# Layer 0's feed-forward in seven block products, and its modulation reductions moved into the two mixers

## The chip, the cores and the metric

One core of one Trainium2 chip runs the whole program. The metric is the time of one execution in microseconds on the device. Beside the runs that are only timed there is one profiled execution, from which every row below is taken.

## The reference, cut to what matters

Two transformer layers work on 640 tokens of 1024 features: 512 tokens of a sample and 128 of a prompt, each with its own modulation. A layer is a mixer and a gated feed-forward, both behind a normalisation that is scaled and shifted by the modulation:

```python
sh, sc, gt, shf, scf, gtf = adaln(silu(c) @ ada_w[layer] + ada_b[layer])   # 6 chunks of 1024, for c and for c_ctx
x = x + gt * mixer(rmsnorm(x) * (1 + sc) + sh)
h = rmsnorm(x) * (1 + scf) + shf
x = x + gtf * ((silu(h @ w_gate) * (h @ w_up)) @ w_down)                   # d_ff = 2816 = 22 slabs of 128
```

Mixer 0 is an S5 recurrence beside neighbourhood attention (four pairs of heads); mixer 1 is a bidirectional Mamba-2 (SSD) in four groups of heads. Everything is in float32.

## The kernel before, in words

A tile framework orders the instructions: every engine and the DMA queue of SyncE (SP) runs its own list in order; the order follows the program's text, with an instruction that could not run yet stepping back behind those that can. SBUF is mostly an arena of twelve blocks (`blk`), two large blocks (`big`), and a weight pool with three slots each of `whi` and `wlo` and two of `wraw`. Matrix products accumulate in PSUM: two double banks `acc` and four single banks `pm`.

A float32 matrix is multiplied as three products of rounded halves. `load_w` (L263) brings a slab of 128 output features over SP's queue, ScalarE rounds it to `whi` (L186), VectorE makes the rest `wlo` (L187), and `gemm` (L278) issues, per 128 inputs, whi by xh, whi by xl and wlo by xh, each in two halves of 320 or 322 columns (L290).

**The modulation** has 96 slabs of 128 features (48 for each layer, 8 to each of the six chunks). The first five chunks of layer 0 are computed on TensorE by `ada_unit` (L218): four steps, each of two 512 KB loads into a `whi` and a `wlo` slot and four float32 matmuls with a stationary tile of 32 columns and 512 moving columns, side by side in the four column groups of the array (two instructions each in the trace). All four steps add into one `pm` bank; then a copy on ScalarE, four transposes and two small additions on VectorE follow. Chunks 2, 3 and 4 of layer 0 run inside mixer 0's attention (`ada_fill`, L1304). The other 56 slabs (chunk 5 of layer 0 and all of layer 1) are computed on VectorE by `ada_tile` (L241): a 512 KB load over SP into a ring of five slots (`adar`, a large block) and two reductions over 1024 elements for each slab (L246), placed in layer 0's feed-forward by `fill` in `build`, two or three slabs for every slab f of gate and up.

**The feed-forward of layer 0** is `ffn` (L393): parts of 8, 7 and 7 slabs. For each f, one gemm of gate and one of up (96 matmuls of 322 columns), the scaling by the row norm (L366), SiLU and product, and the rounding of the result; at a part's end eight gemms with `w_down`, whose result is added to x (`residual`, L381). After the last part's slab m the next norm's work for x[m] follows (`norm_tile`, L335).

**The feed-forward of layer 1** is `ffn_blocks` (L503): parts of 4, 6, 6 and 6. In the first part the products are the plain gemms, and beside them `token_forms` (L433) makes seven combinations of halves of the normalised tokens, rounded in two pieces (`fm`, seven blocks). From f = 4 on, `block_pair` (L460) computes gate and up together from seven products of 128 x 512 weight combinations with those forms: 7 x 4 x 3 = 84 matmuls of 320 columns (L482) for each f.

**Mixer 0's end** (`even_mixer`, L1415): while the fourth pair of heads is in `attention(3)`, the generators `s5_out` (L1182) and `glu` (L1229) are advanced step by step. For each of four feature slabs b, `s5_out` loads `wraw<-kd`, `whi<-fd` and `wlo<-fd`, runs 48 small matmuls, transposes, copies on VectorE to `s5yT`, and a GELU that goes ScalarE, VectorE (L1223), ScalarE, VectorE (L1225), and is rounded to `gh` and `gl`. `glu` is four gemms on those; then the eight gemms with `ev_w_out` follow in `build`.

**Mixer 1** (`odd_mixer`, L901): for each group g, `ssd_group` (L723) yields fourteen times, and `weave` (L846) advances the gemms of the next group (or, in group 3, `ssd_partial`) between them by the digits of `steps`. Nearly every small product of `ssd_group` takes a `pm` bank.

Of the kernel before, what the change touches and what calls it, by code (L numbers as in the profile page):

```python
# [25 lines left out]
FF_PARTS = ((0, 8), (8, 15), (15, 22))  # L26
# [38 lines left out]
def lay_out(a):  # L65
# [5 lines left out]
    d["ada_n"] = np.ascontiguousarray(w[:, :, :5120].reshape(8, 128, 5, 1024).transpose(2, 0, 1, 3))  # L71
    d["cond"] = np.ascontiguousarray(np.broadcast_to(np.stack([a["c"][0], a["c_ctx"]])[None], (128, 2, 1024)))
    d["vecs"] = np.concatenate([fmajor(a[n]) for n, _ in VECS], 1)
    d["ada_w"] = np.ascontiguousarray(a["ada_w"].transpose(0, 2, 1).reshape(96, 128, 1024)[40:])
# [45 lines left out]
class Kernel:  # L120
# [97 lines left out]
    def ada_unit(self, u, pair, row):  # L218
# [16 lines left out]
        m = self.mod[0][:, 8 * u:8 * u + 8].rearrange("p (b j) s -> p b j s", b=2)  # L235
        v = self.vec("ada_b")[:, 8 * u:8 * u + 8].rearrange("p (b j) -> p b j", b=2)
# [12 lines left out]
    def ada(self, layer, tiles):  # L249
        nc = self.nc  # L250
        for j in tiles:
            w = self.adar[:, self.adai % 5]
            self.adai += 1
            nc.sync.dma_start(w, self.I["ada_w"][layer * 48 + j - 40])
            self.ada_tile(layer, j, w)
            if j % 8 == 7:
                self.ada_bias(layer, j - 7, j + 1)
# [135 lines left out]
    def ffn(self, layer, fill=None, after=None):  # L393
        nc = self.nc
        gate = self.mod[layer][:, 40:48]
        for f0, f1 in FF_PARTS:
            nf = f1 - f0
            hh = self.blks("hh", 2, [4, T], F32R)
            hl = self.blks("hl", 2, [4, T], F32R)
            ht = lambda k: (hh[k // 4][:, k % 4], hl[k // 4][:, k % 4])  # L400
            for f in range(f0, f1):
                if fill:
                    fill(f)
                wg = self.load_w(self.I["ffn_w_gate"][layer * NFF + f], 8)
                pg = self.gemm(wg, self.xt, 8, GH)
                wu = self.load_w(self.I["ffn_w_up"][layer * NFF + f], 8)
                pu = self.gemm(wu, self.xt, 8, GH)
                wk = self.blk("ffw", [BLK])
                tg = self.scaled(wk[:, :G], pg)
                tu = self.scaled(wk[:, G:2 * G], pu)  # L410
                sg, hd = wk[:, 2 * G:2 * G + T], wk[:, 2 * G + T:2 * G + 2 * T]
                for s, (a, b, d) in enumerate(SEGS):
                    nc.scalar.activation(sg[:, a:b], tg[:, d:d + b - a], AF.Silu, bias=tg[:, NS + s:NS + s + 1])
                    nc.vector.scalar_tensor_tensor(hd[:, a:b], tu[:, d:d + b - a], tu[:, NS + s:NS + s + 1],
                                                   sg[:, a:b], op0=OP.add, op1=OP.mult)
                self.split(*ht(f - f0), hd)
            last = f1 == NFF
            if last and after is None:
                self.ffn_end(layer, f0, nf, ht)
                return  # L420
            if last:
                after[0]()
            for m in range(8):
                wd = self.load_w(self.I["ffn_w_down"][layer * 8 + m][:, f0 * 128:f1 * 128], nf)
                pd = self.gemm(wd, ht, nf, TH)
                self.residual(self.xk(m), pd, m, gate)
                if last:
                    after[1](m, self.xk(m))
            if last:
                after[2]()  # L430

# [71 lines left out]
    def ffn_blocks(self, layer):  # L503
# [6 lines left out]
        for f0, f1 in ((0, 4), (4, 10), (10, 16), (16, NFF)):  # L510
# [25 lines left out]
            if f1 == NFF:  # L536
                self.ffn_end(layer, f0, nf, ht)
                return
            for m in range(8):
# [1017 lines left out]
```

## Time and profile before

| | us |
|---|---|
| median of 3 runs | 1922.17 (1919.78 to 1922.27) |
| the profiled execution, its own time | 1922.12 |
| its span in the trace | 1920.3 |
| TensorE busy | 1837.2 (96% of the span) |
| VectorE busy | 1342.8 (70%) |
| ScalarE busy | 818.7 (43%) |
| GpSimd busy | 369.6 (19%) |

The profiled execution's own time is 1.8 us above its span, and 0.05 us below the median. The mean granted clock of TensorE over the span is 0.979 of full speed. Matmuls are pipelined: the mean duration of one (some 310 ns for 320 columns) is longer than the distance between two, so distances and windows are the measure of what one costs.

### The profile page before, as it was taken

Reading aid. Unit: us, or ns where it says so; the run is one execution under the profiler, and the core shown is the slowest. Engines: PE = TensorE matmul, PEld = TensorE weight load, DVE = VectorE, ACT = ScalarE, POOL = GpSimd, SP = SyncE. Lnnn points to the kernel's source line nnn. Section 1 sums busy time; section 2 is a strip of 40 time slices with the busy share of each in tenths; the row PEclk is TensorE's granted clock in tenths of the full one; section 3 lists DMA queues with packets and bytes.
Section 4 is the critical chain, followed back from the end, with each engine's and each line's share of the span. In section 5 each row is a group of like instructions: output and inputs, shape, how many; then the busy total and the mean of one; then the engine's idle time right before and its main releaser. Section 6 shows DMA issues by size and latency. Waiting matters only on the chain.

```text
span 1920.3 us, 30941 instructions
## 1 busy us (share of the span) xinstructions
PE 1837.2 (96%) x12340; PEld 1710.7 (89%) x12340; DVE 1342.8 (70%) x2255; ACT 818.7 (43%) x1374; POOL 369.6 (19%) x425
## 2 busy tenths in 40 slices
PE   4899999899999999999999999998999999999997
PEld 1887778899999999999998788875799999999997
DVE  7879933568846856876778696878646876574764
ACT  5454344542212222234655465655444644252442
POOL 1029800010000000012023534346523000000002
PEclk8899999999999999999999999999899999999999
DMA  7355355525434534433221212123422132222222
GB/s 293 119 143 179 114 162 143 216 88 169 156 98 136 163 119 133 157 101 99 93 66 61 77 61 83 57 76 106 134 108 78 39 105 77 82 84 77 94 69 80
DMA packets 102144, 215.82 MB, mean 112 GB/s; under 512 B 15072, under 2 KB 50544, under 8 KB 101488
## 3 DMA queue, kind: packets, MB, share of 16 engines
q1 hardware_dynamic: 101968, 213.83, 34.5%
q8 instruction: 97, 1.59, 0.4%
q14 instruction: 47, 0.39, 0.1%
q0 software_dynamic: 32, 0.02, 0.0%
HBM read 192.31 MB, written 18.84 MB: 110 GB/s over the span
## 4 chain that ended last, share of the span: by engine, by line
PE 82%; DVE 4%; ACT 1%; issue 1%; DMA 1%; DVEq 0%; SPq 0%; ACTq 0%
PE acc L290 59%; PE acc L482 8%; PE pm L482 3%; PE acc L564 1%; PE pm L738 1%; PE pm L564 1%; PE pm L820 1%; DVE ssdw L794 1%; PE pm L1205 1%; PE pm L805 1%; PE pm L787 1%; DVE cv L671 1%; PE acc L1386 1%; PE pm L824 1%; PE pm L226 1%
## 5 line engine op out<-in xcount | busy, mean ns | idle before, releaser
L290 PE MATMUL acc<-xh,whi 128*128 128x322 f32 (+1 forms) x1744 | 417.7, 319 | 8.4 <-ACT xh L1280 6.2
L290 PE MATMUL acc<-xl,whi 128*128 128x322 f32 (+1 forms) x1744 | 416.5, 317 | 0.0
L290 PE MATMUL acc<-xh,wlo 128*128 128x322 f32 (+1 forms) x1744 | 415.9, 317 | 0.0
L186 ACT ACTIVATE whi<-wraw 128x1024 fp32r<-128x1024 f32 (+3 forms) x202 | 204.0, 1011 | 489.1 <-PE acc L290 322.3
L290 PEld LDWEIGHTS acc<-xh,whi 128*128 128x128 f32 x1744 | 296.4, 190 | 24.6 <-issue 14.3
L290 PEld LDWEIGHTS acc<-xh,wlo 128*128 128x128 f32 x1744 | 296.2, 190 | 11.1 <-issue 10.6
L290 PEld LDWEIGHTS acc<-xl,whi 128*128 128x128 f32 x1744 | 297.5, 190 | 8.4 <-issue 7.9
L182 POOL TENSOR_TENSOR ssq<-ssq 128x640 f32<-128x640 f32 (+2 forms) x45 | 71.0, 1577 | 1095.7 <-DMA wraw<-in_ffn_w_down 438.3
L187 DVE TENSOR_TENSOR wlo<-wraw,whi 128x1024 fp32r<-128x1024 f32 (+3 forms) x202 | 242.6, 1202 | 33.0 <-ACT whi L186 32.5
L381 DVE SCALAR_TENSOR_TENSOR x<-acc,mod,x 128x320 f32<-128x320 f32 x168 | 63.4, 434 | 131.3 <-PE acc L290 131.1
L246 DVE CUSTOM_DVE_ANT_0 junk<-adar,cond 128x1024 bf16<-128x1024 f32 x112 | 136.8, 1221 | 1.8
L482 PE MATMUL acc<-fm,whi 128*128 128x320 f32 x576 | 127.5, 309 | 0.0
L671 DVE SCALAR_TENSOR_TENSOR cv<-cv,vecs 128x644 f32<-128x644 f32 x96 | 97.8, 1019 | 15.4 <-ACT cv L669 13.8
L482 PEld LDWEIGHTS acc<-fm,whi 128*128 128x128 f32 x576 | 96.2, 188 | 0.1
L482 PE MATMUL acc<-fm,wlo 128*128 128x320 f32 x288 | 88.8, 309 | 0.0
L290 PE MATMUL acc<-hh,wlo 128*128 128x320 f32 x352 | 79.9, 309 | 0.0
L290 PE MATMUL acc<-hl,whi 128*128 128x320 f32 x352 | 79.8, 308 | 0.0
L290 PE MATMUL acc<-hh,whi 128*128 128x320 f32 x352 | 79.8, 309 | 0.0
L290 PE MATMUL acc<-hb,whi 128*128 128x320 f32 x384 | 72.3, 310 | 2.3 <-DVE fsc L182 1.2
L366 DVE TENSOR_TENSOR ffw<-acc,rext 128x644 f32<-128x644 f32 x52 | 43.1, 828 | 39.2 <-PE acc L290 37.6
L794 DVE SCALAR_TENSOR_TENSOR ssdw<-ssdw,dtk,ssdcb 128x128 f32<-128x128 f32 x160 | 60.4, 441 | 11.2 <-ACT ssdw L792 11.0
L182 POOL TENSOR_TENSOR mt<-s5x,s5co 128x128 f32<-128x128 f32 x79 | 41.7, 537 | 119.3 <-DMA s5x<-in_s5h 114.4
(394 smaller groups left out, 3628.9 us busy)
## 6 DMA issues: line engine op xcount, KB each, us to landing
adar<-in_ada_w SPq DMA_DIRECT2D x56, 512.0 KB, 4.1
wraw<-in_ffn_w_gate SPq DMA_DIRECT2D x44, 512.0 KB, 3.2
wraw<-in_ffn_w_up SPq DMA_DIRECT2D x44, 512.0 KB, 3.3
wraw<-in_od_w_in SPq DMA_DIRECT2D x40, 512.0 KB, 3.2
wraw<-in_ffn_w_down SPq DMA_DIRECT2D x24, 384.0 KB, 3.2
wraw<-in_ev_w_in SPq DMA_DIRECT2D x16, 512.0 KB, 4.1
wraw<-in_od_w_out SPq DMA_DIRECT2D x16, 512.0 KB, 3.6
wlo<-in_ada_n SPq DMA_DIRECT2D x15, 512.0 KB, 5.0
```

Of the source, the lines that this page charges most:

```text
L182: e.tensor_tensor(o, a, b, op=op)
L186: self.nc.scalar.activation(hi, x, AF.Copy)
L187: self.nc.vector.tensor_tensor(lo, x, hi.bitcast(F32), op=OP.subtract)
L226: nc.tensor.matmul(ps[q:q + 32], self.condf[:, 2 * i + a], w[a][:, b * 512:b * 512 + 512], start=i == 0, stop=i == 3)
L246: nc.vector.tensor_tensor_reduce(out=junk, in0=w, in1=self.cond[:, s], scale=1.0, scalar=0.0, op0=OP.mult, op1=OP.add, accum_out=self.mod[ ...
L290: nc.tensor.matmul(ps[:mw, h, :n], a[:, k, :mw], b[:, h * n:(h + 1) * n], start=k0 + k == 0 and q == 0, stop=k0 + k == total - 1 and q == 2)
L366: self.nc.vector.tensor_tensor(t.rearrange("p (h n) -> p h n", h=2), ps[:, :, :GH], self.rext.rearrange("p (h n) -> p h n", h=2), op=OP.mult)
L381: nc.vector.scalar_tensor_tensor(xk[:, a:b], pv, gate[:, m, s:s + 1], xk[:, a:b], op0=OP.mult, op1=OP.add)
L482: nc.tensor.matmul(ps, m[:, k0 + k], x[:, k], start=first and k == 0 and q == 0, stop=k == 3 and q == 2, skip_group_check=not first)
L564: nc.tensor.matmul(ps[:, :n], w[:, k], x[:, a:b], start=k == 0 and q == 0, stop=k == nf - 1 and q == 2)
L671: nc.vector.scalar_tensor_tensor(acc, cb[:, k:k + G], cw[:, k * 24 + wi:k * 24 + wi + 1], acc, op0=OP.mult, op1=OP.add)
L794: nc.vector.scalar_tensor_tensor(E[:, h], E[:, h], self.dt[:, 0, c, g * 8 + h:g * 8 + h + 1], cbs, op0=OP.mult, op1=OP.mult)
```

## The change

The feed-forward of layer 0 becomes `ffn_blocks` too; `ffn` is gone. `ffn_blocks` takes over the `after` hooks (the next norm). The modulation slabs leave the feed-forward: chunk 5 of layer 0 and chunk 0 of layer 1 (16 slabs) go to VectorE during `attention(3)` and `s5_out`, with a ring of two slots in an arena block and with `load_cond` moved there; chunk 1 of layer 1 (8 slabs) goes to VectorE beside the eight gemms with `ev_w_out`, one slab each; chunks 2 to 5 of layer 1 (four units of four steps) go to TensorE in mixer 1's groups 1 to 3.

```diff
-FF_PARTS = ((0, 8), (8, 15), (15, 22))
+FF_PARTS = ((0, 4), (4, 10), (10, 16), (16, 22))
...
-            w = self.adar[:, self.adai % 5]
+            w = self.adar[:, self.adai % self.adar.shape[1]]
...
-    def ffn(self, layer, fill=None, after=None):
...
-    def ffn_blocks(self, layer):
+    def ffn_blocks(self, layer, after=None):
...
+            last = f1 == NFF
+            if last and after is None:
                 self.ffn_end(layer, f0, nf, ht)
                 return
+            if last:
+                after[0]()
             for m in range(8):
                 w = self.load_w(self.I["ffn_w_down"][layer * 8 + m][:, f0 * 128:f1 * 128], nf)
                 self.residual(self.xk(m), self.gemm(w, ht, nf, TH), m, gate)
+                if last:
+                    after[1](m, self.xk(m))
+            if last:
+                after[2]()
...
+        fill = self.ada_fill((3, 4, 2, 5), 1)
+
+        def with_fill(main, at):
+            for i, _ in enumerate(main):
+                if i in at:
+                    next(fill, None)
+                yield
+
         for g in range(4):
             nxt = [self.ssd_in(g + 1)] if g < 3 else [self.ssd_partial()]
-            self.weave(self.ssd_group(g), *([self.ssd_z(g)] if g else []), *nxt, steps=('11111111111112', '11211111111111', '12111111001111', '12011111111101')[g])
+            self.weave(with_fill(self.ssd_group(g), ((), (2, 6, 10), (1, 3, 5, 7, 9, 11), (1, 2, 3, 4, 5, 7, 9))[g]), *([self.ssd_z(g)] if g else []), *nxt, steps=('11111111111112', '11211111111111', '12111111001111', '12011111111101')[g])
+        for _ in fill:
+            pass
...
-        self.af = af = self.blk("af", [4, T])
+        self.af = af = self.blk("af", [3, T])
...
-        fill = self.ada_fill()
+        fill = self.ada_fill((2, 3, 4))
...
         for i, _ in enumerate(self.attention(3)):
             if i < 3:
                 self.split(ah[:, i], al[:, i], af[:, i])
+            if i == 3:
+                self.load_cond()
+                self.adar, self.adai = self.blk("adar", [2, 1024]), 0
+            if i > 3:
+                self.ada(0, range(36 + i, 37 + i)) if i < 12 else self.ada(1, range(0, 1))
             next(fill, None)
             if i > 1:
                 next(out, None)
...
-        self.split(ah[:, 3], al[:, 3], af[:, 3])
-        for _ in out:
-            pass
+        self.split(ah[:, 3], al[:, 3], af[:, 0])
+        for i, _ in enumerate(out):
+            if i < 7:
+                self.ada(1, range(1 + i, 2 + i))
...
         K.load_x()
-        K.load_cond()
         K.adar, K.adai = K.big("adar", [5, 1024]), 0
...
             K.norm_tile(m, K.xk(m))
+            with K.behind(nc.vector):
+                K.ada(1, range(8 + m, 9 + m))
         K.norm_end()
...
-        K.ffn(0, fill=fill,
-              after=(lambda: K.norm_begin(1, "norm_mix_g", 0, 1), keep, K.norm_end))
+        K.ffn_blocks(0, (lambda: K.norm_begin(1, "norm_mix_g", 0, 1), keep, K.norm_end))
```

What is left out moves the weights of layer 1's chunks 2 to 5 into the input layout that `ada_unit` reads, gives `ada_unit` and `ada_fill` a layer, and removes `fill` from `build`.

## Rows read from the trace of the kernel before

**Rows 1.** The page: engines' busy time; the chain that ended last by engine
```profile
PE 1837.2 (96%) x12340; PEld 1710.7 (89%) x12340; DVE 1342.8 (70%) x2255; ACT 818.7 (43%) x1374; POOL 369.6 (19%) x425
PE 82%; DVE 4%; ACT 1%; issue 1%; DMA 1%; DVEq 0%; SPq 0%; ACTq 0%
```

**Rows 2.** Busy time by stretch: engines' busy us (instructions), granted clock, DMA share, GB/s
```profile
240.00:288.00 48.00, 48.00 (x355) 35.74 (x354) 15.60 (x48) 20.51 (x58) 1.76 (x6) 1.00 0.51 163
...
313.00:347.00 34.00, 29.10 (x239) 27.07 (x238) 14.63 (x32) 15.45 (x37) 0.00 (x0) 0.98 0.41 117
347.00:414.63 67.63, 67.63 (x444) 67.50 (x445) 41.98 (x62) 31.15 (x45) 11.75 (x6) 0.96 0.43 158
414.63:884.70 470.07, 470.07 (x3185) 470.06 (x3184) 328.95 (x508) 125.58 (x166) 11.18 (x7) 1.00 0.42 136
1070.00:1176.00 106.00, 102.42 (x643) 86.28 (x643) 86.41 (x133) 62.67 (x99) 46.77 (x35) 0.97 0.21 68
1176.00:1282.00 106.00, 105.84 (x668) 89.78 (x667) 85.59 (x133) 63.08 (x99) 42.45 (x33) 1.00 0.21 68
1282.00:1377.00 95.00, 82.89 (x451) 59.95 (x450) 77.06 (x121) 51.87 (x84) 60.91 (x44) 0.91 0.34 103
1466.02:1555.22 89.20, 87.42 (x595) 86.95 (x594) 67.24 (x127) 45.76 (x87) 4.05 (x2) 1.00 0.21 66
1555.22:1672.52 117.30, 116.57 (x794) 116.07 (x794) 74.52 (x117) 45.35 (x62) 0.00 (x0) 1.00 0.27 86
1672.52:1789.99 117.47, 116.74 (x794) 116.09 (x794) 75.01 (x118) 46.04 (x64) 0.00 (x0) 1.00 0.26 81
```

**Rows 3.** Groups of instructions on VectorE by line: busy us, mean ns | idle before
```profile
L187 DVE TENSOR_TENSOR wlo<-wraw,whi 128x1024 fp32r<-128x1024 f32 (+3 forms) x202 | 242.6, 1202 | 33.0 <-ACT whi L186 32.5
L246 DVE CUSTOM_DVE_ANT_0 junk<-adar,cond 128x1024 bf16<-128x1024 f32 x112 | 136.8, 1221 | 1.8
L381 DVE SCALAR_TENSOR_TENSOR x<-acc,mod,x 128x320 f32<-128x320 f32 x168 | 63.4, 434 | 131.3 <-PE acc L290 131.1
L335 DVE SCALAR_TENSOR_TENSOR xl<-x,amul,xh 128x512 fp32r<-128x512 f32 (+1 forms) x48 | 48.0, 1021 | 5.6 <-ACT xh L334 5.6
```

**Rows 4.** Timeline of TensorE in mixer 0: single steps, a double step, the transposes
```profile
240.82 0.62 PE L226 MATMUL pm<-whi,condf 128*32 128x512 f32 x2
...
241.81 0.56 PE L290 MATMUL acc<-xh,whi 128*128 128x320 f32 x2
...
271.29 0.66 PE L233 MATMUL pm<-ident,whi 128*128 128x128 f32 x4
271.87 0.49 PE L1361 MATMUL pm<-qkv 64*128 64x128 f32 x4
...
283.76 0.62 PE L226 MATMUL pm<-whi,condf 128*32 128x512 f32 x2
...
285.61 0.66 PE L1333 MATMUL pm<-ident,qkv 128*128 128x128 f32 x4
```

**Rows 5.** The chain in group 3 of mixer 1 (1280 to 1380 us), by line
```profile
by line: PE acc L290 30.7%; DVE ssdw L794 13.4%; issue 6.8%; PE pm L820 6.1%; DMA ssq<-yd 5.7%; DVE yl L876 4.5%; DVE ssdw L182 3.4%; PE pm L824 3.1%; DVE wlo L187 2.9%; PE pm L787 2.8%; PE pm L738 2.6%; DVE ssdw L791 2.1%; DVE ssdjk L798 2
```

**Rows 6.** The DMA issues of the page: KB each, median us to landing
```profile
adar<-in_ada_w SPq DMA_DIRECT2D x56, 512.0 KB, 4.1
```

**Rows 7.** Timeline of TensorE: the last reading of the fourth pair's q and k
```profile
312.60 0.49 PE L1361 MATMUL pm<-qkv 64*128 64x128 f32 x4
```

**Rows 8.** The chain at the end of mixer 0, in order of time: start us, us
```profile
340.48 2.25 issue
342.74 0.74 ACT wraw L1222
343.50 0.84 DVE wraw L1223
344.37 0.74 ACT wraw L1224
345.13 0.84 DVE s5yT L1225
345.99 0.74 ACT gh L186
346.78 3.30 PE acc L290 x11
```

**Rows 9.** What SP's queue waited for, 280 to 345 us: total, times, longest
```profile
SPq L1192 <- DVE s5yT L1225: 15.3, 2, 9.6
```

**Rows 10.** Timeline of ScalarE and VectorE: the SiLU of `cond`; layer 0's second row norm
```profile
372.40 1.92 ACT L193 ACTIVATE cond<-cond 128x2048 f32<-128x2048 f32 x1
...
423.11 0.19 DVE L348 RECIPROCAL rs<-sd 128x5 f32<-128x5 f32 x1 [4.35 <-ACT sd L346]
```

More of the change, by code (lines that the diff above doesn't have):

```diff
@@ L70, in lay_out @@
     w = a["ada_w"][0].reshape(8, 128, 6144)
-    d["ada_n"] = np.ascontiguousarray(w[:, :, :5120].reshape(8, 128, 5, 1024).transpose(2, 0, 1, 3))
+    units = lambda z: z.reshape(8, 128, -1, 1024).transpose(2, 0, 1, 3)
+    d["ada_n"] = np.concatenate([units(w[:, :, :5120]), units(a["ada_w"][1][:, 2048:])], 0)
     d["cond"] = np.ascontiguousarray(np.broadcast_to(np.stack([a["c"][0], a["c_ctx"]])[None], (128, 2, 1024)))
     d["vecs"] = np.concatenate([fmajor(a[n]) for n, _ in VECS], 1)
-    d["ada_w"] = np.ascontiguousarray(a["ada_w"].transpose(0, 2, 1).reshape(96, 128, 1024)[40:])
+    d["ada_w"] = np.ascontiguousarray(a["ada_w"].transpose(0, 2, 1).reshape(96, 128, 1024)[40:64])
     for n in ("ffn_w_gate", "ffn_w_up"):
@@ L216, in ada_stage, with ada_unit @@
                 self.w0 = self.raw_w(self.I["ev_w_in"][0], 8)
-    def ada_unit(self, u, pair, row):
+    def ada_unit(self, u, pair, row, layer=0):
         nc = self.nc
@@ L234, in ada_unit @@
         part = pt.rearrange("p (j a b x) -> p a b j x", j=4, a=2, b=2)
-        m = self.mod[0][:, 8 * u:8 * u + 8].rearrange("p (b j) s -> p b j s", b=2)
-        v = self.vec("ada_b")[:, 8 * u:8 * u + 8].rearrange("p (b j) -> p b j", b=2)
+        m = self.mod[layer][:, 8 * u:8 * u + 8].rearrange("p (b j) s -> p b j s", b=2)
+        v = self.vec("ada_b")[:, 48 * layer + 8 * u:48 * layer + 8 * u + 8].rearrange("p (b j) -> p b j", b=2)
         nc.vector.tensor_tensor(m, part[:, 0, :, :, :2], v[:, :, :, None].to_broadcast([128, 2, 4, 2]), op=OP.add)
@@ L390, in xk @@
         return self.x[:, k]
-    def ffn(self, layer, fill=None, after=None):
[L394 to L430, printed above, removed]
     def token_forms(self, layer, xs):
@@ L509, in ffn_blocks @@
         ht = lambda k: (hb[:, 0, k], hb[:, 1, k])
-        for f0, f1 in ((0, 4), (4, 10), (10, 16), (16, NFF)):
+        for f0, f1 in FF_PARTS:
             nf = f1 - f0
@@ L535, in ffn_blocks @@
                     self.split(*ht(f - f0), self.block_pair(layer, f, sc, ws, wd[:, f % 2]))
-            if f1 == NFF:
+            last = f1 == NFF
+            if last and after is None:
                 self.ffn_end(layer, f0, nf, ht)
                 return
+            if last:
+                after[0]()
             for m in range(8):
@@ L1302, in qkv, with ada_fill @@
             yield
-    def ada_fill(self):
+    def ada_fill(self, units, layer=0):
         slot = lambda n: self.wpool.tile([128, 8, 128], F32, name=n).rearrange("p k m -> p (k m)")
@@ L1310, in of @@
                 for a in range(2):
-                    self.nc.sync.dma_start(w[a], self.I["ada_n"][u, 2 * i + a])
+                    self.nc.sync.dma_start(w[a], self.I["ada_n"][u + 3 * layer, 2 * i + a])
                 return w
             return of
-        for u in (2, 3, 4):
-            yield from self.ada_unit(u, pair(u), lambda: slot("whi")[:, :512])
+        for u in units:
+            yield from self.ada_unit(u, pair(u), lambda: slot("whi")[:, :512], layer)
     def load_bias(self, p):
@@ L1409, in attention @@
                 yield
-        o = self.af[:, p]
+        o = self.af[:, p % 3]
         wr = lambda z: z.rearrange("p (w r) -> p w r", r=8)
@@ L1511, in keep @@
             nc.sync.dma_start(xd[:, m], xk)
-        def fill(f):
-            a = [min(q, 8) * 12 // 8 + max(q - 8, 0) * 36 // 14 for q in (f, f + 1)]
-            with K.behind(nc.vector):
-                if f < 8:
-                    K.ada(0, range(40 + f, 41 + f))
-                K.ada(1, range(*a))
-        K.ffn(0, fill=fill,
-              after=(lambda: K.norm_begin(1, "norm_mix_g", 0, 1), keep, K.norm_end))
+        K.ffn_blocks(0, (lambda: K.norm_begin(1, "norm_mix_g", 0, 1), keep, K.norm_end))
         K.odd_mixer()
```

## The prediction

> **What bounds the kernel now.** I read the page first, for which engine to count: TensorE is busy 96% of the span and makes 82% of the chain that ended last, VectorE 4% of it [rows 1]. So a change is worth what it takes from TensorE, and costs what it puts there or what makes TensorE wait. Then I cut the span into the stretches that the change touches [rows 2]; in each the reader compares TensorE's busy time with the length, and looks at how much of VectorE is free. Layer 0's feed-forward runs from its first 322-column matmul at 414.63 to the first one of mixer 1 at 884.70, and TensorE is busy in all of it. Mixer 1's groups 1 to 3 lie at about 1070 to 1176, 1176 to 1282 and 1282 to 1377: TensorE idles 3.6, 0.2 and 12.1 us there, and in the last the clock is 0.91 of full speed. Mixer 0's end (313 to 347) has 4.9 us of idle, one wait at its very end [rows 8]. Third come the chains and the waits in mixer 1's last group and at mixer 0's end [rows 5, 8, 9].
>
> **Part A: layer 0's feed-forward.** For 18 of the 22 slabs f, 96 matmuls become 84: 216 fewer. Layer 1 runs the very same code in this trace, so I take whole stretches instead of counting instructions: first part 89.20 us, then 117.30 and 117.47 for parts of six slabs and their eight down gemms [rows 2]. Layer 0's last part also has 6 x 84 + 8 x 36 = 792 matmuls, taken as 117.4. Sum 441.4 against 470.07 before: **-28.7 us**. Counted by matmul it is 216 x 470.07/3185 = 31.9 us; the 3 us between are the small stalls of the block products, which I keep. What could spoil the last part is the next norm's work, which layer 1 does not have there: for each down slab VectorE has three additions of 0.43, one remainder of 1.20 and two norm pieces of 1.02 [rows 3], 4.5 us, beside 36 matmuls of 0.147, 5.3 us. It is hidden, with 0.8 us to spare; eight times a miss of as much as 0.6 us would cost 5. So A lies between -32 and -24. The eight extra down slabs (24 more additions, eight more loads and roundings) are in layer 1's stretches. The 48 slabs of loads and 96 reductions (1.22 us each) that leave the feed-forward [rows 3, 6] give nothing back, since TensorE never waited in it.
>
> **Part B: sixteen steps on TensorE in mixer 1.** A step between other matmuls takes from 240.82 to 241.81, 0.99 us; two in a row take 283.76 to 285.61, 0.93 each; a unit's four transposes take 0.58 [rows 4]. So 16 x 0.99 + 4 x 0.58 = 18.1 us of TensorE. Three steps fall in group 1, six in group 2 and seven in group 3. Groups 1 and 2 are full, so nine steps and two sets of transposes, 10.1 us, come out as time, less some of the 3.6 us of idle at group 1's start; say 9. In group 3 VectorE's products stand on the chain beside TensorE [rows 5] and 12.1 us are idle; I let half of the 8.1 us vanish: 4. **+13 us**. The bounds: 2 if all 15.9 us of idle in the three groups are filled, about 27 if the idle nearly doubles. Below nothing is excluded, as nothing there is removed. The 32 loads of 512 KB go through SP and wait for a `whi` or `wlo` slot; behind them stand the loads of `od_w_in`, asked for a product or two ahead. DMA is 0.21 to 0.34 busy there [rows 2]. A step holds one of three slots; with two, the rounding of the next slab (about 2.2 us, 1.20 of them on VectorE [rows 3]) still fits beside the 7.1 us of a 48-matmul gemm. Without that cover a step would cost up to 2.2. The copy on ScalarE and two additions per unit are under 1 us and lie beside the gemms.
>
> The steps use 32 columns of the array between matmuls that use 128. The rows show both switches inside the 0.99, 0.06 more than a step in a pair [rows 4]. The Trainium skill, "TensorEngine Tiling (Array Packing)", Key Properties, says that changing the tiling mode drains the TensorE. With a drain as long as a whole matmul lasts, some 0.31 us as told with the profile, the 32 switches would make 10 us more and the result 1924; the row has the switch in it and decides, so I give this no chance of its own.
>
> **Part C: mixer 0's end and the output gemms.** Sixteen slabs x 2 reductions x 1.22 us [rows 3] = 39 us of VectorE are added before 347, and eight slabs, 19.5 us, beside the output gemms. When can they begin? Of twelve blocks, eleven are held when the ring is asked for (u, the fourth pair's qkv and bias, two for attention, af, ah, al, yT, gh, gl); `cond` takes the twelfth, so the ring waits for qkv, last read at about 313 [rows 7]. From 313 to 347 VectorE is free 34 - 14.6 = 19.4 us, and from 347 to 414.63 25.6 [rows 2]: 45.0 free for 58.6 asked. So 13.6 us too much, even perfectly packed. It may slide into the next feed-forward's first part, where 22 of 89.2 us are free [rows 2]. But the sixteen come ahead of the last GELU and of `glu` in the program, so they go first when both are ready. A two-slot ring also paces them: 4.1 us to landing [rows 6] plus 2.4 on VectorE, over two slots, gives 3.3 us a slab, so sixteen take 53 us, from 313 to 366, past the last GELU (342 to 347). Each of that chain's VectorE pieces [rows 8] can then find a reduction running, 1.22 us, or two; so can `glu`'s. With four such pieces in the last GELU and about three in `glu` that TensorE awaits, at 1.2 us each, I take **+8 us**. The bounds: 0 if the order lets them past (less is excluded: nothing is taken out), and 22 if all of the 39 - 19.4 = 20 us must end first, with 1.9 us of ScalarE for the SiLU of `cond` [rows 10]. SP gets 17 loads more there; a load of the ring waits for the reductions two slabs back, and behind it on SP stand the `kd` loads of `s5_out`, which already wait 15.3 us for VectorE [rows 9], and the output weights. That is the path by which a late reduction reaches TensorE sooner than by the GELU.
>
> The last of the eight slabs, behind the last norm tile, lies in the 4.35 us for which VectorE waits before the row norm's reciprocal [rows 10]; without that cover it costs 2.4 us.
>
> **Sum.** The profiled execution took 1922.1, 1.8 above its span and 0.05 below the median. 1922.1 - 28.7 + 13 + 8 = **1914.4 us**.
>
> **Rivals.** (1) Slower: VectorE is the bound at mixer 0's end, and the last GELU waits for the reductions. For it: 45.0 free against 58.6, and the order of the program. Against it: most of the S5 matmuls need no VectorE, and a list ordered by readiness lets a GELU piece in between two slabs. Price C = 22: 1922.1 - 28.7 + 13 + 22 = 1928.4. It decides from C above 15.7, where B and C eat A. (2) No change: a unit holds one of four `pm` banks from its first step to its transposes, and with sixteen steps spread over three groups one bank is gone nearly throughout; group 3's chain of small products then waits more. Price: half of the 15.9 us of idle on top, B = 21: 1922.4. Against it: mixer 0 held a bank the same way at 240 to 288, with attention beside it, and TensorE was busy in all 48 us [rows 2]. The Trainium skill, "Perfetto Trace Analysis", Matmul Optimizations, asks that all eight PSUM banks be used; by it this rival gains, and no row here shows three banks in mixer 1. (3) Better: group 3's idle takes all of its seven steps (B = 5, since group 1 hides its three too) and the reductions slip past the GELU (C = 4): 1902.4. That the change does not do what it says I exclude: the block code runs in layer 1 and the units in mixer 0.
>
> **How the numbers follow.** A measurement of this kernel can tell about 0.2%, 3.8 us, from no change. Forecast 0.46, rival 3 0.20, rival 1 0.20, rival 2 0.14. The forecast's own range is 1906 to 1922, so 0.03 of it falls within 0.2%; with most of rival 2 that makes 0.15. Faster: 0.43 + 0.20 = 0.63. The rest, 0.22, is rival 1 and a little of rival 2. The range reaches to rivals 1 and 3, 1901 to 1929, which leaves out about half of rival 1 and a third of rival 3.
>
> **What the changed profile would show.** A: a stretch of 441 us between the first 322-column matmul after the output gemms and the first of mixer 1, with TensorE idle under 5 us in it; more would be VectorE in the last part. B: the three groups, 307 us before, at about 320; TensorE waiting on ScalarE or VectorE before `pm` products in group 3 well beyond 12 us speaks for rival 2, and waits for a `whi` DMA for the slots. C: the last GELU 6 to 8 us later, with reductions between its VectorE pieces; 20 us later is rival 1. The forecast is wrong if the stretches from 313 to 414.63 grow by more than 16 us, or the groups by less than 6 or more than 20.

## The result and the profile after

The changed kernel took **1932.9 us** (median of 4 runs, 1931.0 to 1939.1) against 1921.3 for the kernel before, run in turn with it: a ratio of 1.0067, 95% interval 1.0041 to 1.0092. It is slower, by 11.6 us, where 1914.4 was forecast, and it lies outside the range of 1901 to 1929. The profiled execution, 1931.0 us, is the shortest of the four; the changed kernel's rows are from it.

The page of the changed kernel, as in [rows 1]:

```profile
PE 1825.8 (95%) x12268; PEld 1675.5 (87%) x12268; DVE 1362.6 (71%) x2345; ACT 893.1 (46%) x1509; POOL 367.6 (19%) x425
PE 83%; DMA 2%; DVE 2%; ACT 1%; issue 1%; POOL 0%; SPq 0%; DVEq 0%; ACTq 0%
```

TensorE lost 11.4 us of work, and the span grew from 1920.3 to 1929.1: so it does less and stands still for longer. Where, is read from the same first products as in the forecast, three lines of TensorE's timeline of the changed kernel (start us, us):

```profile
428.80 0.47 PE L291 MATMUL acc<-xh,whi 128*128 128x322 f32 x2
...
868.92 0.45 PE L291 MATMUL acc<-xh,whi 128*64 128x322 f32 x2
...
1475.30 0.46 PE L291 MATMUL acc<-xh,whi 128*128 128x322 f32 x2
```

Before, these stood at 414.63, 884.70 and 1466.02 [rows 2]. So the way to layer 0's feed-forward is 14.2 us longer, the feed-forward 29.95 shorter (440.12 for 470.07), mixer 1 25.1 longer (606.38 for 581.32), and the rest 0.5 shorter: +8.8, the whole difference of the spans.

Busy time by stretch, changed kernel, columns as in [rows 2]: mixer 0's end in three, layer 0's feed-forward in its four parts, mixer 1's groups 1 to 3:

```profile
288.00:336.00 48.00, 42.84 (x330) 33.90 (x328) 35.88 (x82) 22.73 (x60) 0.00 (x0) 1.00 0.82 251
336.00:384.00 48.00, 36.75 (x233) 35.72 (x232) 36.92 (x69) 17.97 (x29) 0.00 (x0) 0.86 0.70 239
384.00:428.80 44.80, 44.80 (x308) 44.80 (x307) 44.59 (x66) 17.56 (x28) 12.27 (x6) 1.00 0.36 118
428.80:518.00 89.20, 88.32 (x601) 88.07 (x600) 68.64 (x135) 47.46 (x86) 0.00 (x0) 1.00 0.21 67
518.00:635.30 117.30, 116.57 (x793) 116.08 (x793) 75.39 (x120) 46.29 (x63) 0.00 (x0) 1.00 0.26 85
635.30:752.80 117.50, 116.77 (x796) 116.27 (x795) 73.47 (x116) 44.79 (x63) 0.00 (x0) 1.00 0.26 81
752.80:869.00 116.20, 115.47 (x786) 114.96 (x786) 84.44 (x129) 55.30 (x84) 11.09 (x11) 1.00 0.31 100
1054.00:1160.00 106.00, 102.42 (x625) 80.33 (x626) 79.78 (x125) 65.07 (x99) 39.68 (x32) 0.98 0.29 93
1160.00:1276.00 116.00, 115.19 (x731) 91.49 (x727) 85.94 (x143) 62.87 (x98) 47.04 (x35) 1.00 0.35 118
1276.00:1390.00 114.00, 99.94 (x579) 69.66 (x578) 78.85 (x130) 56.76 (x92) 62.48 (x45) 0.93 0.47 152
```

Three things are to be seen. The feed-forward's parts are layer 1's [rows 2] to within 1.2 us. In mixer 1 TensorE's idle time is what it was: 3.6, 0.8 and 14.1 us against 3.6, 0.2 and 12.1; nothing has been filled. At mixer 0's end TensorE idles 16.4 us between 288 and 384, while the DMA engines are 0.82 and 0.70 busy.

What began there, in the timeline of SP's queue:

```profile
279.95 0.35 SPq L193 DMA_DIRECT2D cond<-in_cond  x1
281.93 0.43 SPq L255 DMA_DIRECT2D adar<-in_ada_w  x1
285.84 6.04 SPq L1175 DMA_DIRECT2D wlo<-fd  x2
...
331.04 0.38 SPq L1459 DMA_DIRECT2D wglu<-in_s_w_glu  x1
```

and in VectorE's (in brackets the idle time before, and what ended it):

```profile
290.75 1.23 DVE L247 CUSTOM_DVE_ANT_0 junk<-adar,cond 128x1024 bf16<-128x1024 f32 x1 [11.91 <-DMA adar<-in_ada_w]
291.90 1.14 DVE L183 TENSOR_TENSOR af<-acc,attw 128x512 f32<-128x512 f32 x2
```

and, in the kernel before, at the same place:

```profile
287.37 1.18 DVE L182 TENSOR_TENSOR af<-acc,attw 128x512 f32<-128x512 f32 x2 [8.33 <-PE acc L1386]
```

The ring did not wait until 313: it was granted at 282, just ahead of the loads of `fd`, and its first slab took 8.7 us to land. VectorE stood 11.9 us before the first reduction, and the attention's `af` products behind it began at 291.90; before, at 287.37. Most of the 11.9 us it had no work in the kernel before either (8.3 us), so the wait for the slab delayed it by 4.5 us. The chain at the end of this stage in the changed kernel, against [rows 8]:

```profile
354.10 4.44 DMA adar<-in_ada_w
358.67 1.23 DVE junk L247
359.90 0.75 DVE s5yT L1204
360.67 0.75 ACT gh L187
361.46 4.55 PE acc L291 x15
```

The last GELU waits for a reduction, and that one for its slab's transfer; the product behind it comes 14.7 us later than before, where 6 to 8 were forecast.

### The profile page after: what moved, and what is told of

The parts are those of the page before. It is cut to its first block, busy times and chain, and to the rows that moved or that the text cites. A ratio compares the mean times of both kernels' runs of the same rounds, so it can differ in the third digit from the quotient of the medians.

```text
span 1929.1 us, 31117 instructions
## 1 busy us (share of the span) xinstructions
PE 1825.8 (95%) x12268; PEld 1675.5 (87%) x12268; DVE 1362.6 (71%) x2345; ACT 893.1 (46%) x1509; POOL 367.6 (19%) x425
## 4 chain that ended last, share of the span: by engine, by line
PE 83%; DMA 2%; DVE 2%; ACT 1%; issue 1%; POOL 0%; SPq 0%; DVEq 0%; ACTq 0%
PE acc L291 46%; PE acc L444 16%; PE pm L444 7%; PE pm L774 2%; PE pm L227 1%; PE pm L707 1%; PE acc L533 1%; PE pm L533 1%; PE pm L789 1%; PE pm L756 1%; PE pm L1184 1%; DMA adar<-in_ada_w 1%; PE acc L1365 1%; PE pm L793 0%; DMA ssq<-yd 0%
## 5 line engine op out<-in xcount | busy, mean ns | idle before, releaser
L187 ACT ACTIVATE whi<-wraw 128x1024 fp32r<-128x1024 f32 (+2 forms) x192 | 186.3, 973 | 317.8 <-PE acc L291 217.6
L291 PE MATMUL acc<-xh,whi 128*128 128x322 f32 (+2 forms) x1168 | 284.3, 322 | 8.3 <-ACT xh L1259 6.2
L291 PE MATMUL acc<-xl,whi 128*128 128x322 f32 (+2 forms) x1168 | 283.0, 320 | 0.0
L291 PE MATMUL acc<-xh,wlo 128*128 128x322 f32 (+2 forms) x1168 | 281.3, 319 | 0.3 <-DVE wlo L188 0.2
L188 DVE TENSOR_TENSOR wlo<-wraw,whi 128x1024 fp32r<-128x1024 f32 (+2 forms) x192 | 221.3, 1154 | 39.4 <-ACT whi L187 39.2
L291 PEld LDWEIGHTS acc<-xh,whi 128*128 128x128 f32 (+1 forms) x1168 | 197.2, 190 | 26.4 <-issue 13.9
L291 PEld LDWEIGHTS acc<-xl,whi 128*128 128x128 f32 (+1 forms) x1168 | 198.8, 190 | 11.3 <-issue 10.9
L291 PEld LDWEIGHTS acc<-xh,wlo 128*128 128x128 f32 (+1 forms) x1168 | 197.8, 189 | 11.8 <-issue 10.5
L291 PEld LDWEIGHTS acc<-hb,whi 128*128 128x128 f32 x896 | 140.1, 188 | 8.4 <-DVE fsc L183 4.2
L444 PE MATMUL pm<-fm,whi 128*128 128x320 f32 x576 | 128.1, 308 | 0.0
```

The lines of the kernel that those rows point to most:

```text
L187: self.nc.scalar.activation(hi, x, AF.Copy)
L188: self.nc.vector.tensor_tensor(lo, x, hi.bitcast(F32), op=OP.subtract)
L291: nc.tensor.matmul(ps[:mw, h, :n], a[:, k, :mw], b[:, h * n:(h + 1) * n], start=k0 + k == 0 and q == 0, stop=k0 + k == total - 1 and q == 2)
L444: nc.tensor.matmul(ps, m[:, k0 + k], x[:, k], start=first and k == 0 and q == 0, stop=k == 3 and q == 2, skip_group_check=not first)
```

## The experiments

The way to the pair of `ada_unit` steps near 283.6 us [rows 4] differs between profiles by up to 7 us, whatever the kernel, with the granted clock between 150 and 240 us (0.87 to 0.94), so the price at mixer 0's end is read from that pair to the feed-forward's first product: 130.9 us before (283.76 to 414.63), 145.25 in the changed kernel. A stretch is read from one profile of each run, and what it can tell is bounded by profiles that do the same work in it. Four have the changed kernel's work at mixer 0's end (it, e1, e4 and e5): 145.3, 145.5, 147.5 and 145.3 us. Seven without these sixteen slabs (before, e2, e3, e7, v5, v6, v8) have 130.6 to 131.0. So with slabs a difference of some 2 us says nothing. The times of e4, e5, e7, f1, f2, f4 and f6 are of one execution each.

**Each placement taken away, and both.** e1:

```diff
-        fill = self.ada_fill((3, 4, 2, 5), 1)
+        nc.vector.memset(self.mod[1][:, 16:48], 0.5)
+        fill = iter(())
```

> Left out: layer 1's mod chunks 2 to 5 (a constant stands in their place); the rest is the changed kernel. If the sixteen steps on TensorE are all of the 25.1 us by which mixer 1 grew, the stretch from mixer 1's first state product to layer 1's first feed-forward product goes from 606.4 back to 581.3 us and the time to 1932.9 - 25.1 = 1907.8 us. Rival: mixer 1 is longer for another reason too (what ffn_blocks leaves behind, another place of blocks); then the stretch stays at 588 us or more and the time at 1914 or more, since only the 18.1 us of the forecast's own step sum would go.

e2 leaves out `load_cond`, the ring and the sixteen `ada` calls in `even_mixer` and puts `load_cond` back into `build`:

> Left out: the sixteen slab reductions at the end of mixer 0 with their loads (chunk 5 of layer 0 and chunk 0 of layer 1 become constants; the conditioning is loaded after the mixer as in the kernel before). If these are all of the 14.2 us lost up to the first feed-forward product, it comes at 414.6 us as before instead of 428.8 and the time is 1932.9 - 14.2 = 1918.7 us. Rival: the eight slabs beside the output products cost part of it (they were not there before); then it comes at 417 us or later, and the time is 1921 or more.

e3 is both:

> Both left out at once: no steps on TensorE in mixer 1 and no slabs at the end of mixer 0. What stays is the feed-forward of layer 0 in block products. If the three parts add up, the time is 1932.9 - 25.1 - 14.2 = 1893.6 us, that is 28 to 30 us below the kernel before. If the two placements hinder one another (or the gain of the feed-forward depends on one of them), it differs from that sum by more than 3 us.

| run | median us | ratio to before, interval | pair to product | feed-forward 0 | mixer 1 |
|---|---|---|---|---|---|
| e1, no steps | 1911.0 | 0.9933, 0.9915 to 0.9951 | 145.5 | 440.1 | 581.6 |
| e2, no slabs | 1914.6 | 0.9952, 0.9936 to 0.9969 | 130.6 | 439.8 | 602.6 |
| e3, neither | 1893.6 | 0.9852, 0.9828 to 0.9875 | 130.8 | 439.8 | 582.7 |

The parts add up: 39.3 us less without both, 21.9 and 18.3 alone. The feed-forward's gain of 30 us stands by itself, the eight slabs beside the output products (still there in e2) cost nothing, and mixer 1's growth is the steps'. How much they cost varies: the ten profiles here with all sixteen full steps have 601.2 to 606.5 us, mean 603.4, and the five without any 581.3 to 583.4, mean 582.4. That is 19 to 24 us, 21 on the mean. The changed kernel's 606.4 is at the upper end; eight of the ten are at 604.3 or below.

**Why the steps come out in full.** e5 keeps the matmuls and drops the loads; e4 keeps the held bank, makes the matmuls small, and drops the loads and the transposes:

```diff
-            w = pair(i)
+            w = pair(i) if layer == 0 else None
...
-                    nc.tensor.matmul(ps[q:q + 32], self.condf[:, 2 * i + a], w[a][:, b * 512:b * 512 + 512], start=i == 0, stop=i == 3)
+e5                  nc.tensor.matmul(ps[q:q + 32].rearrange("p (i n) -> p i n", i=4), self.condf[:, 2 * i + a], self.ident[:, None].to_broadcast([128, 4, 128]), start=i == 0, stop=i == 3)
+e4                  nc.tensor.matmul(ps[q:q + 32, :16], self.condf[:, 2 * i + a], self.ident[:, :16], start=i == 0, stop=i == 3)
```

> The sixteen steps in mixer 1 keep all matmuls and transposes at full size but read a resident tile, so that the 32 loads of 512 KB into the weight slots are gone and no weight tile is given up for them (the results of these chunks are thereby other numbers). If TensorE's own time is the price, mixer 1 stays at about 606 us (within 3). If the slots and loads are, it falls to 588 to 592 us, or by the time of the waits on them alone (2.8 us shown) to 603.

> In mixer 1 each of the sixteen steps still takes and holds its pm bank from the unit's first step to its end, but its matmuls have 16 columns instead of 512, read a resident tile, and the transposes are gone (chunks 2 to 5 of layer 1 become other numbers). If TensorE's time for the steps is the price, mixer 1 falls from 606.4 to 585 to 589 us (581.6 to 582.7 without any step, plus the 256 short matmuls). Rival, the held bank: it stays at 594 us or more, half of the 25 us or over.

e5: mixer 1 606.5 us, time 1931.1: loads and slots cost nothing. e4: 586.9 us, 1914.7. Busy time over mixer 1, each kernel's first line to last product, first without steps (e1), then the changed kernel, then e4:

```profile
873.90:1455.51 581.61, 565.07 (x3557) 493.30 (x3554) 436.14 (x645) 310.83 (x497) 228.70 (x182) 0.98 0.26 83
```

```profile
868.92:1475.30 606.38, 586.90 (x3701) 496.09 (x3699) 430.52 (x655) 315.55 (x503) 226.21 (x182) 0.98 0.32 107
```

```profile
872.23:1459.16 586.93, 570.26 (x3685) 495.97 (x3682) 436.28 (x651) 314.67 (x499) 226.82 (x182) 0.98 0.25 82
```

TensorE's busy time grows by 21.8 us, its idle time from 16.5 to 19.5. With the banks held and hardly any work the idle time is 16.7: the held bank is no price, and most of e4's 5 us are its short matmuls (0.19 us a step by its timeline, 3 in all). The Trainium skill, "Perfetto Trace Analysis", Matmul Optimizations, asks for all eight banks; here one fewer for most of a stage cost 2.6 us at most (586.9 - 581.3, less the 3.0 of the matmuls).

A step, in the changed kernel's timeline of TensorE, at full clock and at the low one:

```profile
1078.05 0.62 PE L227 MATMUL pm<-whi,condf 128*32 128x512 f32 x2
...
1079.05 1.12 PE L707 MATMUL pm<-ssdw,ssdbc 128*128 128x512 f32 x2
...
1319.52 1.92 PE L227 MATMUL pm<-whi,condf 128*32 128x512 f32 x4 [2.81 <-DMA whi<-in_ada_n]
1321.37 0.79 PE L756 MATMUL pm<-ssdr,ssdl 32*128 32x512 f32 x2
1322.09 1.92 PE L227 MATMUL pm<-wlo,condf 128*32 128x512 f32 x4
```

One is 1.00 us among 128-column matmuls, as in mixer 0 [rows 4]. The step at 1319.52 is the exception: its `whi` and its `wlo` matmuls came one after the other instead of side by side, 1.85 us each, where the granted clock was 0.57 (1318 to 1326 us). Sixteen at 1.00 and four sets of transposes at 0.58 are 18.3. The rest of the price, 0.5 to 6 us, is not explained: that one wait and that one step are no reason for it, since e5 has neither and its mixer 1 is as long, with TensorE busy for 590.3 us of it.

**What costs at mixer 0's end.** f1 keeps the loads and shrinks the reductions; f2 keeps the reductions and drops all but the first two loads (`adai` is counted up before it is asked; the expectations of f2 and f4 say three); f4 does both; f6 is f1 with loads of 16 columns:

```diff
+        n = 16 if layer == 0 or j < 8 else 1024
-out=junk, in0=w, in1=self.cond[:, s],
+out=junk[:, :n], in0=w[:, :n], in1=self.cond[:, s, :n],        (f1, f4, f6)
+            if layer and j > 7 or self.adai < 3:               (f2, f4)
                 nc.sync.dma_start(w, self.I["ada_w"][layer * 48 + j - 40])
```

> At the end of mixer 0 and beside the output products all slab loads stay, but each reduction reads 16 columns instead of 1024 (the two layers' chunks become other numbers), so that VectorE loses nearly all of the 58 us added there while the transfers and their order on SP stay. Measured from the step pair near 283.6 to the feed-forward's first product: 145.3 us in the changed kernel, 130.8 without the slabs. If the VectorE work is the price (my forecast's reason), 131 to 135 us; if the loads on SP's queue and their share of the DMA are, 141 to 146.

> The counterpart: all reductions at full size, but only the first three slabs are loaded at the end of mixer 0, the other reductions read what lies in the ring (those chunks become other numbers). From the step pair near 283.6 to the feed-forward's first product: if VectorE's work is the price, 142 us or more of the 145.3; if the loads are, 131 to 135 (130.8 without slabs). A value between, on both runs, says that the two share it.

> Of the work at the end of mixer 0 hardly anything is left: three slab loads, reductions of 16 columns (both layers' chunks become other numbers). What stays are the two blocks that the conditioning and the ring hold from 280 us to the end of the output products, and the conditioning's load and SiLU. Step pair near 283.6 to the feed-forward's first product: 130.8 without slabs, 145.3 in the changed kernel, 145.5 with the loads alone, 140.3 with the reductions alone. If the price is the blocks (wglu's load waits about 9 us for one on SP, with the kd loads behind it), 138 to 143 us here too. If loads and reductions are each a price of their own, 131 to 134.

> As in the run with the loads alone (reductions of 16 columns), but each of the sixteen slab loads brings 16 columns instead of 1024: the same number of loads, with the same waits for the ring and the same place on SP's queue, and 1/64 of the bytes (both layers' chunks become other numbers). Step pair near 283.6 to the feed-forward's first product: 145.5 with the full loads, 133.8 with three loads only. If the bytes are the price (DMA engines full from 283 to 313 when the S5 output maps are fetched), 132 to 136 us. If it is what waits behind a slab load on SP, or the order of the list that the scheduler makes with these instructions in it, 141 to 146.

| run | slab loads | reductions | pair to product us | TensorE idle in it | time us |
|---|---|---|---|---|---|
| e3 | none | none | 130.8 | 6.5 | 1893.6 |
| f4 | 2 | 16 columns | 133.8 | 8.5 | 1918.6 |
| f6 | all, 1/64 of the bytes | 16 columns | 137.0 | 9.9 | 1919.8 |
| f2 | 2 | full | 140.3 | 13.5 | 1926.0 |
| f1 | all | 16 columns | 145.5 | 15.9 | 1927.7 |
| changed kernel | all | full | 145.3 | 18.0 | 1932.9 |

(All but e3 have mixer 1's steps.) f4's 3.0 us come with the wait for the first slab and the two blocks held, which no run separates; its `af` products begin 7.0 us after the pair, 3.6 in e3. In f6 they begin at 6.7, and the first slab, of 8 KB there, took 7.6 us to land: its own bytes are not what made it late. That the blocks are the price, the first of the two readings offered for f4, fell. From there the reductions add 6.5 and the loads 11.6, of which 8.4 go when the bytes go. Both together add 11.4, no more than the loads alone. So the transfers, which the forecast priced at nothing beyond the ring's pace, are the larger part, and enough for all of it. The first 30 us, in f1 and then in f6:

```profile
283.75:313.75 30.00, 24.17 (x158) 15.71 (x158) 7.66 (x47) 13.38 (x32) 0.00 (x0) 0.94 1.01 316
```

```profile
284.65:314.65 30.00, 25.03 (x164) 16.48 (x162) 10.87 (x73) 14.25 (x34) 0.00 (x0) 0.93 0.75 209
```

With the slabs in full the DMA engines are busy without a gap (1.01, 316 GB/s), with VectorE free for 22 of the 30 us; without the bytes they are at 0.75, as in e3 (0.74). But TensorE idles nearly as much in these 30 us in f6 as in f1, 5.0 and 5.8 us (1.6 in e3). What sets the two apart comes later, in TensorE's waits in f1 and, below, in the changed kernel (us in total, times, longest):

```profile
PE acc L292 <- ACT whi L187: 5.5, 1, 5.5
PE acc L292 <- ACT gh L187: 3.8, 1, 3.8
```

```profile
PE acc L291 <- ACT gh L187: 6.8, 1, 6.8
PE pm L1182 <- DMA wraw<-kd: 3.0, 1, 3.0
```

In f1 the first `glu` product waits for `wglu`, which is issued 48.9 us after the pair (36.6 in f6, 28.2 in e3) and takes 9.2 us to land; in the changed kernel a `kd` load and then the last GELU are waited for. In f6, f4 and e3 the only wait of over 2 us is the last GELU's, 4.9 us in each.

**The same loads on another queue, and `wglu` ahead of them.** f3 issues the sixteen loads with `nc.gpsimd.dma_start`; f5 moves the lines that allocate and load `wglu` from i == 9 to i == 3, ahead of `load_cond`.

> The changed kernel with one thing moved: the sixteen slab loads at the end of mixer 0 are issued on the GpSimd queue, which is empty there, instead of SP's, where the loads of kd and fd and of the output weights stand behind them. Step pair near 283.6 to the feed-forward's first product: 145.3 us on SP's queue, 130.8 without slabs. If the price is that a slab load waiting for its ring slot holds up what stands behind it on SP, 132 to 138 us and a time of about 1920 to 1926; if it is the bytes themselves (the DMA engines are full from 283 to 313), or the VectorE work, 142 us or more and 1930 to 1934.

> The changed kernel in full, but wglu takes its block, and is loaded, ahead of the conditioning and the ring, so that these wait for the next block that comes free and wglu no longer waits on SP with the kd loads behind it. Step pair near 283.6 to the feed-forward's first product: if wglu's wait for a block is the price, 131 to 137 us and a time of 1918 to 1925; if the slabs' own work and bytes are, 143 us or more and 1930 to 1934; the ring that starts later may also push its reductions into the last GELU, as my forecast had it, for 138 to 141.

f3: 147.0 us and 1929.7 (ratio 1.0034, 1.0024 to 1.0044). What stands behind a slab on SP is not the price by itself. The Trainium skill, "Trainium Kernel Development and Optimization", Key Constraints, says that transfers issued from SP, ScalarE and GpSimd share the same 16 DMA engines; this run agrees, with the engines 0.99 busy in the first 30 us where they were 0.98 on SP's queue. f5: 143.3 us and 1930.0 (1.0041, 1.0027 to 1.0055): `wglu`'s wait for a block is worth 2 us, the size of the scatter. In f3 `wglu` still waits 9.1 us for its block, and in f5 the slabs are still on SP; both at once was not tried.

**In search of a better placement.** Seven versions, all but e7 with nothing left out:

```diff
+v9   for p in range(3): ...  if p == 2 and i == 1: self.load_cond(); self.adar, self.adai = self.blk("adar", [2, 1024]), 0
+v10  the same, and fill = self.ada_fill((3, 4, 2), 1); K.ada(1, range(40 + m, 41 + m)) beside od_w_out
+v3   fill = chain(self.ada_fill((2, 3, 4)), self.ada_fill((0, 1), 1)) at i in (1, 3, 5, 7, 9, 11); chunk 5 of each layer beside its mixer's output products
+v5   ffn_blocks: fsc 1, self.load_cond(); after each block_pair self.ada(1, ...), 40 slabs, ring: tiles whi, wlo
+v6   as v5, ring loads on nc.gpsimd, chunk 5 as steps
+e7   neither steps nor slabs, fsc 1
+v8   as v6, parts of four slabs, no hc, fsc 2
```

> The changed kernel in full with one thing moved: the conditioning and the sixteen slabs of mixer 0 start one head pair earlier, from about 240 us, where the DMA engines are 0.35 busy, VectorE is free for about 20 of each 30 us and TensorE is the bound, instead of at 282, where the S5 output maps fill the DMA engines. If the slabs' bytes on top of the maps are the price of the 14.5 us, the feed-forward's first product comes 3 to 7 us later than without slabs instead of 14.5, and the time is 1922 to 1927. If it is any sixteen slabs beside attention (VectorE in order, blocks held), or if the blocks are not free so early and SP stands still for them, it stays at 1932 or gets longer.

> As that version, and besides chunk 5 of layer 1 goes from four steps on TensorE in mixer 1 to eight slabs beside mixer 1's output products, with the ring in the half of ssdx that is free there. If the early slabs cost 3 to 7 us and four steps less save 4 to 6: 1893.6 + 3 to 7 + 15 to 19 = 1912 to 1920, which would be below both kernels. If the slabs again run into layer 1's feed-forward, its end is 14 to 19 us longer than the 453.8 us it has now, and the time 1927 or more.

> Nothing left out; another placement of the modulation work with the same feed-forward. Chunk 5 of layer 0 on VectorE beside the output products of mixer 0, chunk 5 of layer 1 on VectorE beside those of mixer 1 (both places cost nothing if the slabs beside the output products are hidden), chunks 0 and 1 of layer 1 as steps on TensorE in mixer 0's attention (two steps where there was one), chunks 2 to 4 in mixer 1 (12 steps instead of 16). From the 1893.6 us without either placement: 12 steps at 1.2 to 1.55 us in mixer 1, 15 to 19 us, and 8 steps in mixer 0 at 0 to 1.2 us, 0 to 10: 1908 to 1922 us. If a slab beside mixer 1's output products is not hidden, up to 19 us more.

> Nothing left out; all modulation slabs on VectorE, none on TensorE and none at the end of mixer 0: chunk 5 of layer 0 beside mixer 0's output products (shown to be hidden there), chunks 0 to 4 of layer 1 beside layer 0's block products (40 slabs, 80 reductions of 1.22 us, 98 us, where VectorE is free for 118 us; the block products' second scratch block goes to the conditioning, the ring is the weight slots), chunk 5 of layer 1 beside mixer 1's output products. If VectorE's free time there can be used as it lies, 1893.6 plus up to 10 us: 1894 to 1904. If the reductions make the block products wait (each of 18 waits for one or two of them, 1.2 to 2.4 us, or the single scratch block serialises), 20 to 45 us more: 1915 to 1938.

> Nothing left out. As the version with all slabs on VectorE, with two things mended: the 40 slabs' loads beside layer 0's block products go out on the GpSimd queue, which is empty there, so that SP's weight loads no longer stand behind a wait for a ring slot (98.7 us of such waits before), and chunk 5 of layer 1 is four steps on TensorE in mixer 1 instead of slabs that ran into layer 1's feed-forward. Layer 0's feed-forward: 440 us without slabs, 481 with them on SP. If the blocked queue was the price, 443 to 452; if the reductions between the block products' own VectorE pieces, or the single scratch block, are, 465 us or more. Mixer 1: 581.6 plus 4 steps at 1.2 to 1.5, 587 to 589. Time: 1903 to 1912 in the first case, 1925 to 1945 in the second.

> Neither steps nor slabs (as in the run that leaves both out, chunks are constants), and layer 0's block products have one scratch block instead of two. Layer 0's feed-forward: 440 us with two. If the single scratch block is what made the two versions with slabs on VectorE 41 to 43 us longer there, 470 us or more; if the reductions among the block products' own VectorE work are, 440 to 450.

> Nothing left out. As the last version (40 slabs beside layer 0's block products, loads on the GpSimd queue, 4 steps in mixer 1), but the conditioning takes the block of the fifth and sixth hidden slab instead of a scratch block, so that layer 0's feed-forward goes in parts of four slabs (six parts, 16 more down slabs with three additions of 0.43 us each) and keeps both scratch blocks. Feed-forward of layer 0, 483 in the last version: if the scratch block was the price, 445 to 455 and a time of 1908 to 1920; if VectorE is (241 us of its own plus 98 of reductions plus about 21 for the added down slabs, in 359), 475 to 490 and 1940 to 1957.

| version | median us | ratio, interval | what it shows |
|---|---|---|---|
| v9 | 1930.6 | 1.0045, 1.0030 to 1.0060 | the ring's block came free at 273, not 240: 146.5 us, nothing saved |
| v10 | 1946.2 | 1.0128, 1.0112 to 1.0144 | twelve steps, mixer 1 still 609.4; end 463.2 for 453.8 |
| v3 | 1946.5 | 1.0123, 1.0099 to 1.0147 | eight steps more in mixer 0: product at 433.4, 413.9 in e3; end 472.9 |
| v5 | 1951.6 | 1.0152, 1.0135 to 1.0169 | feed-forward 481.2 |
| v6 | 1950.5 | 1.0145, 1.0127 to 1.0163 | feed-forward 483.0 |
| e7 | 1899.7 (one run) | | feed-forward 446.4 |
| v8 | 1960.5 | 1.0201, 1.0182 to 1.0221 | feed-forward 492.0 |

None of the six that leave nothing out beats the kernel before. In v3, v5 and v10 chunk 5's slabs beside mixer 1's output products ran on into layer 1's feed-forward (its end 472.9, 468.3 and 463.2 us). v6 and v8 keep four steps in mixer 1, 4.6 us by the sum above and 587 to 589 us expected for mixer 1; it took 596.7 and 593.9, where v5, with no step, took 583.4. So the price does not follow the number of steps: four cost 12 to 14 us above the mean without any, twelve 17 in v3, sixteen 19 to 24. What is paid beyond the steps' own time was not found. Beside the block products (v5, v6, v8) 118 us of VectorE are free and 98 were asked, and the stage got 41 to 52 us longer; the single scratch block of v5 and v6 is 6.6 of them (e7), SP's queue none (v6). TensorE's waits there in v5, 518 to 880 us:

```profile
PE acc L447 <- ACT whi L187: 9.9, 9, 1.6
PE pm L447 <- ACT whi L187: 5.2, 5, 1.7
PE pm L447 <- ACT fsc L457: 5.1, 9, 0.6
PE acc L447 <- DVE fsc L183: 3.8, 7, 1.7
```

Many waits of under 2 us, for rounded weights above all. That the ring in the weight slots is their cause was not tried apart.

## Why the prediction was wrong

**A was right.** 441.4 forecast, 440.1 measured, and 439.8 to 440.1 in e1 to e3. (What leaves the feed-forward is all 56 slabs and 112 reductions [rows 3], not 48 and 96; the time does not depend on it.) The last part took 116.2 for 117.4, so the next norm's work is hidden there, as argued. The eight slabs beside the output products are hidden too (e2), the last in front of the reciprocal included.

**B failed at one step: "In group 3 ... 12.1 us are idle; I let half of the 8.1 us vanish: 4"**, and with it the few microseconds of group 1. The step's own price, 18.1 us, was right (18.3); none of it vanished, and mixer 1 paid 25.1 in this profile and 21 on the mean of ten, above the 20 named as the bound of being right. What the runs show in its place: the 12.1 us of idle were still there, 14.1, and over all of mixer 1 idle went from 16.5 to 19.5 us while the busy time grew by 21.8; neither the loads (e5) nor the held bank (e4) are the price. My explanation, which no run tests apart, is that idle time of TensorE in a chain is time in which the next product has not got its operands yet: a step put on the queue between two products of that chain delays the one behind it, and the operands of all that follow come later by as much. It does not explain why mixer 1 pays more than the 18.3, nor the 12 to 14 us of four steps in v6 and v8. The upper bound was also off: B = 27 is an idle time that grows by 9 us; nearly doubled it would be 34. Rival 2, the held bank, has the size of the mean, 21, and the wrong cause (e4). The drain that the Trainium skill, "TensorEngine Tiling (Array Packing)", Key Properties, tells of shows no further price: the step takes 1.00 us between full-width matmuls in mixer 1 too.

**C failed at the step "so the ring waits for qkv, last read at about 313", and in what it priced.** The count of blocks was off: the ring had its block at 282, and `wglu` waited in its stead. That put the slabs into the stretch where the `fd` loads already keep the DMA engines 0.74 busy (e3 and before). Of the 14.4 us, 3.0 are there with two slabs and hardly any reduction (f4), with VectorE standing before the first slab and the attention's pieces behind it; all the loads, without the reductions' time, bring as much as the two together, and 8.4 of their 11.6 go with their bytes; the reductions, on which the forecast rested, bring 6.5 by themselves. A transfer was priced only as the ring's pace, 4.1 us to landing [rows 6]; here the first took 8.7, and what the other loads lost by it was not in the sum. Rival 1 had the right side by another mechanism; by its own reckoning C had to pass 15.7, with B at this profile's 25 even the 8 us forecast for C would have made the kernel some 3 us slower, with B at its mean of 21 it would have been 1 or 2 us faster: no change that can be told.

So the sum was -30.0 + 25.1 + 14.2 - 0.5 = +8.8 in the profile where it was to be -28.7 + 13 + 8 = -7.7. What is left open is what mixer 1 pays beyond the steps' own time, why the reductions alone cost 6.5, and how far the price of the bytes is the lateness of the `fd`, the `kd` or the `wglu` loads or of the slabs themselves.

## What to carry to other kernels

Work put on the bounding engine cost its whole time and more here, in a stage where that engine idles too (18.3 us of steps: 19 to 24); count it in full unless it is shown that it can run inside a wait without standing in front of the product that ends it. When work moves to another engine, price its transfers in the stretch where they will fall, against what the DMA engines carry there, before the engine that computes. An engine that takes its list in order and waits for a transfer holds what is queued behind it: the attention's products came 4.5 us later here, behind a reduction of 1.2 us that waited for its slab.

## What was not expected

The loads without the reductions' time (145.5 us), the reductions with two loads (140.3) and both (145.3) do not add: a stage with 6.5 us of idle time on its bound goes to 13.5 to 18 by any of them. The stretches in which TensorE idled also show the low clock: from pair to product the mean granted clock is 0.97 without slabs and 0.95 with them, and between 336 and 384 us 0.86. Idle time grew by 11.5, so some 3 of the 14.4 us are matmuls that ran slower. And the free VectorE time beside TensorE's block products, 118 us of 351, was no free place: 98 us of reductions made that stage 41 to 52 us longer.
